# Dilated attention in an encoder block: values loaded and multiplied once per item, weights of both heads in one transfer, two buffers for the statistics' rows

## The chip, the cores and the metric

The kernel runs on one core of a Trainium2 chip. The metric is the device time of one execution in microseconds (us); before the change it is 1399.53 us, the median of three runs (1398.49 to 1399.57). The core has these engines, each with its own queue of instructions that it works through in order: PE (matmul, with PEld for its weight loads), DVE and ACT (elementwise work; they alone evacuate PE's results from PSUM), POOL (elementwise work in SBUF), and SP, which in this kernel issues nearly all transfers. The transfers themselves are carried by 16 DMA engines.

## The reference, cut to what matters

The block has three mixers. The change touches only the dilated attention: 24 heads in three groups of eight, with dilations 1, 4 and 16, and a softmax over the groups' log-denominators that weighs the three outputs of a head.

```python
A_GROUPS = ((128, 1), (512, 4), (2048, 16))
...
for gi, (window, dil) in enumerate(A_GROUPS):
    hs = slice(gi * A_HEADS, (gi + 1) * A_HEADS)
    o_g, lse_g = dilated_window_attention(aq[:, :, hs], ak[:, :, hs], av[:, :, hs], window, dil)
    outs.append(o_g)
    lses.append(lse_g)
wts = jax.nn.softmax(jnp.stack(lses, axis=0), axis=0).astype(dt)
oa = jnp.einsum('gbsh,gbshd->bshd', wts, jnp.stack(outs, axis=0)).reshape(b, s, BRANCH_WIDTH)
...
ya = (oa * jax.nn.silu(ga)) @ w_br_a[layer]
```

Inside a group a query sees a band of keys of its own residue class: 64 positions on either side for dilations 1 and 4, the whole class (64 positions) for dilation 16. There are 1024 tokens and 64 numbers per head.

## The kernel before

Everything before about 1060 us (projections, the other two mixers, rotary positions) leaves q, k and v of the dilated attention in device memory: `qkd` holds q and k with heads in pairs, `vdr` the values. The change lies in the stage that follows.

**Items and visits.** The eight heads of a group are worked in four pairs `p_`. An *item* is one pair in one group, so there are 12, in the order of `seq`: pair 0 with groups 0, 1, 2, then pair 1, and so on; items are counted from 0 in this document, so that item 5 is pair 1, group 2, and item 7 is pair 2, group 1. (Pair 0 has items 0 to 2.) The 1024 queries are eight tiles of 128, `T`, worked two at a time in four *visits* `b`. After each visit come two short steps `rest(T)` for `T` = 2b and 2b+1. An item is thus: visit 0, rest 0, rest 1, visit 1, rest 2, rest 3, visit 2, rest 4, rest 5, visit 3, rest 6, rest 7. The text calls these rests T0 to T7.

**What a visit does.** It computes on PE the scores of its two tiles (`scores`, L1567, L1571, L1579), on DVE the mask and the row minimum (L1591) and on ACT the exponential with its sum (`soft`, L1592). Two visits later PE transposes these probabilities (`trans`, L1614) and DVE copies them out of PSUM (L1620), so visits 0 and 1 of an item transpose tiles of the item before (`pre`). When half an item has been transposed, `pv` multiplies it with the values (L1635 for group 2, L1645 and, for the band's edges, L1655 for the others), and ACT moves the result into the tile `og` (L1665). This happens for `pre` in visits 0 and 2.

**Values.** `values(x)` loads one half of an item's values into the single tile `vfull` (named avs in the profile; L1516, L1520, L1524) right behind the `pv` that has read the item before out of that half. `turned_values` loads the copies with the other half of the partitions (avt; L1535, L1536, L1540) at T1. The last of them (L1536) exists because tile 4 of group 0 needs tile 3's values after that half has been overwritten.

**Statistics and weights.** In visit 1 `stats` turns the row minima and sums of `pre` (L1672) and ACT copies them to `sr` (one buffer; L1675, L1677, L1679); at T3 `send` writes them to device memory (`std`; L1687, L1691, L1694). When the three groups of a pair are done, `combine` puts 14 steps on the list `todo`; `STEP_T` says at which T each is taken, over the next three items: fetch the statistics (cpt, L1793), compute the shares, the weights, `put` them to `wgd` (L1818), load those of groups 0 and 1 back, broadcast over 64 partitions a head (`load`, wgt, L1788), multiply and add on POOL (`weigh`, L1826 and L1824), load group 2's and the gate (L1833), multiply and add, gate (L1829), store (L1837) or keep. This is done for pairs 0, 1 and 2: their `put` and first loads are at T3 of items 4, 7 and 10. Pair 3 is finished otherwise (`shares_3`, `ending`), from rows that are loaded at T2 and T4 of item 11 (L1727).

**Beside it.** Between the visits PE works on the y units (`add_y`, L1891): the gated output projections of the other two mixers. Their weights are loaded by SP (L1337), copied by ACT (L1342) and split on POOL (`y_split`, L1343); the gates' tiles come by L1350 and their evacuation is on DVE. The order on each engine is the order in which the program issues, and `weave` sets it from written costs that do not change here. Items 8 and 9 also load a finished part of the first branch (`dl_load`, hl, L1865, at T5), which ACT copies in the next item at T0 and T1 (`dl_high`, L1869).

**Buffers.** `vfull` has one, `wgt` two, `og` five, the probabilities (pra) five, their transposes (app) four, q and k two each. In PSUM the scores have two banks, transposes and `pv` and the statistics share four in rotation, the y units two.

Of the kernel before, what the change touches and what calls it, by code (L numbers as in the profile page):

```python
# [8 lines left out]
F32 = mybir.dt.float32  # L9
# [6 lines left out]
S = 1024  # L16
# [17 lines left out]
def block(ctx: ExitStack, tc: tile.TileContext, x, xT, memT, cst, msk, bcst, tabA, gpost,  # L34
# [174 lines left out]
    std = dram.tile([4, 3, 2, 2, S], F32, name="std")  # L209
    wgd = dram.tile([4, 2, 3, S], F32, name="wgd")  # L210
    tsd = dram.tile([4, 4, P, 512], F32, name="tsd")
# [1259 lines left out]
    with ExitStack():  # L1471
# [24 lines left out]
        def item(p_, g):  # L1496
# [5 lines left out]
            def place(T, h):  # L1502
                return h ^ (T // 2 % 2 if g == 2 else T % 2)

            def sides(T):
                return [not x for x in edges(g, T)]

            def values(x):

                v = vdr[g, p_]  # L1510
                if g == 2:
                    vv = v.rearrange("(u r) f -> u r f", r=16)
                    for o in range(2):
                        for h in range(2):
                            T = 4 * x + 2 * o
                            nc.sync.dma_start(vfull[hf[h ^ o], T:T + 2].rearrange("p b z d -> p (b z) d"),  # L1516
                                              vv[:, 2 * T:2 * T + 4, hf[h]])
                    return
                if g == 0:
                    nc.sync.dma_start(vfull[:, 4 * x:4 * x + 4].rearrange("p b h d -> p b (h d)"),  # L1520
                                      v[512 * x:512 * x + 512].rearrange("(b q) f -> q b f", q=128))
                else:
                    for e in range(2):
                        nc.sync.dma_start(vfull[:, 4 * x + e:4 * x + 4:2].rearrange("p b h d -> p b (h d)"),  # L1524
                                          v.rearrange("(u r) f -> u r f", r=4)[128 * e:128 * e + 128, 2 * x:2 * x + 2])

            def turned_values():

                v = vdr[g, p_]
                vturn = d["vt"] = aa.tile([P, 8, 64], F32, name="avt", bufs=2)  # L1530
                if g == 0:
                    vb_ = v.rearrange("(b k) f -> k b f", k=64)
                    for y, t0, t1, b0, h in ((0, 1, 8, 1, 1), (0, 2, 7, 3, 0), (1, 0, 7, 2, 1), (1, 1, 6, 4, 0)):
                        m = (t1 - t0 + 1) // 2
                        nc.sync.dma_start(vturn[hf[y], t0:t1:2], vb_[:, b0:b0 + 4 * m - 3:4, hf[h]])  # L1535
                    nc.sync.dma_start(vturn[hf[1], 7], v[448:512, hf[1]])  # L1536
                else:
                    vc = v.rearrange("(u r) f -> u r f", r=4)
                    for y in range(2):
                        nc.sync.dma_start(vturn[hf[y], 1 - y:8 - y:2], vc[64 + 64 * y:128 + 64 * y, :, hf[1]])  # L1540

            def value_of(T, h, side):

                y = place(T, h)
                vturn = d["vt"]
                if y == side:
                    return vturn[hf[y], T]
                if (g, T, side) == (0, 4, 0):
                    return vturn[hf[1], 7]
                return vfull[hf[y], T + (1 if side else -1), h]  # L1550
# [71 lines left out]

            def pv(b):
                if b == 0:
                    d["og"] = OG[p_, g] = cb.tile([P, S], F32, name="og", bufs=5)
                og = d["og"]
                ov = [pst().rearrange("p a b -> p (a b)") for _ in range(2)]
                if g == 2:
                    for j in range(2):
                        for z in range(2):  # L1630
                            for o in range(2):
                                T = 4 * b + 2 * o + j
                                for h in range(2):
                                    y, c = hf[place(T, h)], 128 * j + 64 * z
                                    PE.matmul(ov[o][hf[h], c:c + 64], vfull[y, T, z], st[T][y, z, 64 * j:64 * j + 64],  # L1635
                                              start=True, stop=True)
                    views = [(og.rearrange("p (u r) -> p r u", r=16)[:, 8 * b + 4 * o:8 * b + 4 * o + 4],
                              ov[o][:, 0:256].rearrange("p (r u) -> p r u", r=4)) for o in range(2)]
                else:
                    for i in range(2):  # L1640
                        for e in range(2):
                            T = 4 * b + 2 * i + e
                            for h in range(2):
                                c = 64 + 128 * e + 64 * place(T, h)
                                PE.matmul(ov[e][hf[h], 128 * i:128 * i + 128], vfull[:, T, h], st[T][:, :, c:c + 64],  # L1645
                                          start=i == 0, stop=False)
                    for i in range(2):
                        for r in range(2):
                            for e in range(2):
                                T = 4 * b + 2 * i + e  # L1650
                                if not sides(T)[r]:
                                    continue
                                for y in range(2):
                                    h, c = place(T, y), 128 * i + 64 * r
                                    PE.matmul(ov[e][hf[h], c:c + 64], value_of(T, h, r), st[T][hf[y], r, 320 * e:320 * e + 64],  # L1655
                                              start=False, stop=i == 1 and (r == 1 or not sides(T)[1]))
                    views = []
                    for e in range(2):
                        if g == 0:
                            dst = og[:, b * 512:b * 512 + 512].rearrange("p (i e q) -> p e i q", i=2, e=2)[:, e]  # L1660
                        else:
                            dst = og.rearrange("p (u r) -> p r u", r=4)[:, 2 * b:2 * b + 2, 128 * e:128 * e + 128]
                        views.append((dst, ov[e][:, 0:256].rearrange("p (i q) -> p i q", i=2)))
                for dst, src in views:
                    A.activation(dst, src, AF.Copy)  # L1665
                for T in range(4 * b, 4 * b + 4):
                    st.pop(T)

            def stats():
                sts = d["sts"]  # L1670
                tp = pst()
                PE.transpose(tp[0:32, 0, :], sts.rearrange("p h s t -> p (h s t)"), ident)  # L1672
                sr = cb.tile([32, 128], F32, name="sr", bufs=1)
                if g == 0:
# [26 lines left out]
        def plan(it, pre, nxt):  # L1701
# [77 lines left out]
        def combine(p_, ogs):  # L1779
# [5 lines left out]
            def load(g):  # L1785
                wgt[g] = cb.tile([P, S], F32, name="wgt", bufs=2)
                for h in range(2):
                    E.dma_start(wgt[g][h * 64:h * 64 + 64], wgd[p_, h, g:g + 1].to_broadcast([64, S]))  # L1788
# [27 lines left out]
            def put():  # L1816
                for h in range(2):
                    E.dma_start(wgd[p_, h].rearrange("g (i e) -> i g e", e=16), c["w"][h * 64:h * 64 + 64])  # L1818

# [530 lines left out]
```

## Time and profile before

The program was profiled in an execution of its own, which took 1399.23 us; its span, from the first to the last instruction, is 1397.1 us.

| what | before |
|---|---|
| median of 3 runs | 1399.53 us |
| profiled execution, its time and its span | 1399.23 us, 1397.1 us |
| issues of values (L1516, L1520, L1524) | 32, 8, 16 |
| issues of turned values (L1535, L1536, L1540) | 16, 4, 8 |
| issues of weights, shares, put (L1788, L1793, L1818) | 18, 6, 6 |
| `og` evacuations on ACT (L1665) | 48 of 128x256 |

How to read the profile: times are us from the start of the span. In the row of an engine on a page, busy time is followed by its share of the span and the number of instructions. A row of waits reads "who waited <- who ended the wait: us in total, times, longest us"; in a row of SP's own waits, SPq is its queue. A row of the timeline reads "start, duration, engine, line, operation, out<-in", and x4 at its end says that four alike were merged. A row of windows has, for each stretch, its length, the busy time of PE, PEld, DVE, ACT and POOL with the number of instructions, the granted share of PE's clock, the busy share of the 16 DMA engines and the GB/s that they moved. A group's row has "busy us, mean ns | idle time before it and what ended it". Tile names are the program's.

### The profile page before, as it was taken

Reading aid. Unit: us, or ns where it says so; the run is one execution under the profiler, and the core shown is the slowest. Engines: PE = TensorE matmul, PEld = TensorE weight load, DVE = VectorE, ACT = ScalarE, POOL = GpSimd, SP = SyncE. Lnnn points to the kernel's source line nnn. Section 1 sums busy time; section 2 is a strip of 40 time slices with the busy share of each in tenths; the row PEclk is TensorE's granted clock in tenths of the full one; section 3 lists DMA queues with packets and bytes.
Section 4 is the critical chain, followed back from the end, with each engine's and each line's share of the span. In section 5 each row is a group of like instructions: output and inputs, shape, how many; then the busy total and the mean of one; then the engine's idle time right before and its main releaser. Section 6 shows DMA issues by size and latency. Waiting matters only on the chain.

```text
span 1397.1 us, 22991 instructions
## 1 busy us (share of the span) xinstructions
PE 1365.4 (98%) x8303; PEld 1093.4 (78%) x8303; DVE 1016.2 (73%) x1840; ACT 658.2 (47%) x1408; POOL 579.4 (41%) x443
## 2 busy tenths in 40 slices
PE   7999999999999999999999999999999998899997
PEld 7799987666666789988888888888887776668886
DVE  7768667777776598767778776677777666568977
ACT  6454455656655345333333333433336775553332
POOL 0507702676666100245555553465651243552003
PEclk9999999999999999999999999999999999999999
DMA  6355532322243688424223333333338777876455
GB/s 234 103 183 199 186 114 99 101 77 91 75 139 135 216 249 251 156 83 128 92 98 113 117 110 111 117 121 113 105 128 275 218 199 209 243 198 218 142 198 181
DMA packets 126354, 213.88 MB, mean 153 GB/s; under 512 B 33345, under 2 KB 65441, under 8 KB 126241
## 3 DMA queue, kind: packets, MB, share of 16 engines
q1 hardware_dynamic: 116928, 198.49, 44.5%
q10 hardware_dynamic: 9312, 13.93, 2.8%
q8 instruction: 65, 1.06, 0.3%
q14 instruction: 49, 0.39, 0.1%
HBM read 145.99 MB, written 66.38 MB: 152 GB/s over the span
## 4 chain that ended last, share of the span: by engine, by line
PE 87%; DMA 4%; POOL 3%; DVE 2%; ACT 2%; issue 1%; SPq 1%; DVEq 0%; POOLq 0%; ACTq 0%
PE s L1309 35%; PE d L1891 5%; PE s L1219 4%; PE s L2115 4%; PE ov L804 4%; PE sc L2033 3%; PE d L128 3%; PE d L130 3%; PE d L132 3%; PE s L1270 3%; PE tr L770 2%; PE s L789 2%; PE s L788 2%; PE d L2115 2%; PE d L523 1%; DMA wgt<-wgd 1%
## 5 line engine op out<-in xcount | busy, mean ns | idle before, releaser
L795 POOL TENSOR_TENSOR bl<-bl,bp 128x512 f32<-128x512 f32 x96 | 133.0, 1385 | 54.1 <-ACT bp L791 48.6
L1309 PE MATMUL s<-hh,vS 128*128 128x512 f32 x400 | 133.4, 395 | 0.0
L1309 PE MATMUL s<-vA,vS 128*128 128x512 f32 x450 | 106.6, 390 | 0.0
L91 DVE TENSOR_TENSOR vS<-vot,vS 128x512 fp32r<-128x512 f32 x75 | 86.4, 1153 | 19.9 <-ACT vS L90 19.9
L1309 PEld LDWEIGHTS s<-vA,vS 128*128 128x128 f32 x450 | 84.5, 188 | 18.3
L791 ACT ACTIVATE bp<-s 128x512 f32<-128x512 f32 x128 | 75.7, 596 | 43.8 <-PE s L789 42.7
L771 DVE TENSOR_REDUCE bn<-tr 128x1 f32<-128x512 f32 x128 | 85.0, 684 | 13.7 <-PE tr L770 12.5
L128 PE MATMUL d<-hh,wh 128*128 128x512 f32 x224 | 90.1, 402 | 2.4 <-DVE fth L201 2.4
L1592 ACT ACTIVATE pra<-pra,sts 128x192 f32<-128x192 f32 (+1 forms) x176 | 72.8, 415 | 39.2 <-DVE sts L1591 39.0
L132 PE MATMUL d<-hh,wl 128*128 128x512 f32 x224 | 89.9, 402 | 0.0
L130 PE MATMUL d<-hl,wh 128*128 128x512 f32 x224 | 89.4, 399 | 0.0
L1309 PEld LDWEIGHTS s<-hh,vS 128*128 128x128 f32 x400 | 75.3, 188 | 17.7
L1620 DVE COPY app<-tr 128x320 f32<-128x320 f32 (+2 forms) x96 | 37.8, 435 | 59.1 <-PE tr L1614 59.1
L1309 PE MATMUL s<-hl,vS 128*128 128x512 f32 x200 | 79.1, 395 | 0.0
L1309 PE MATMUL s<-hh,wh 128*128 128x512 f32 x200 | 78.4, 392 | 0.0
L1309 PE MATMUL s<-hh,wl 128*128 128x512 f32 x200 | 78.4, 392 | 0.0
L1309 PE MATMUL s<-hl,wh 128*128 128x512 f32 x200 | 77.8, 389 | 0.0
L1313 ACT ACTIVATE vv<-s 128x512 f32<-128x512 f32 x50 | 30.0, 599 | 85.5 <-PE s L1309 59.0
L1053 POOL TENSOR_TENSOR vot<-wr 128x512 f32<-128x512 f32 x13 | 22.2, 1706 | 111.9 <-DMA wr<-in_wu 111.9
L804 PE MATMUL ov<-bp,VS 128*64 128x512 f32 x256 | 58.5, 598 | 0.0
L1053 POOL TENSOR_TENSOR vot<-vot,vA 128x512 f32<-128x512 f32 x12 | 19.3, 1609 | 90.6 <-DVE vS L91 90.6
L128 PEld LDWEIGHTS d<-hh,wh 128*128 128x128 f32 x224 | 42.6, 190 | 16.2 <-issue 5.5
(627 smaller groups left out, 4042.3 us busy)
## 6 DMA issues: line engine op xcount, KB each, us to landing
wr<-in_wu SPq DMA_DIRECT2D x40, 512.0 KB
vA<-in_wu SPq DMA_DIRECT2D x24, 512.0 KB
qkd<-ko SPq DMA_DIRECT2D x96, 128.0 KB
wl<-thd SPq DMA_DIRECT2D x24, 512.0 KB
wos<-os SPq DMA_DIRECT2D x12, 512.0 KB
wr<-in_wbr SPq DMA_DIRECT2D x24, 256.0 KB
aq<-qkd SPq DMA_DIRECT2D x12, 512.0 KB
ak<-qkd SPq DMA_DIRECT2D x12, 512.0 KB
```

What stands on the lines that cost most here:

```text
L91: V.tensor_tensor(dst_l, src, dst_h.bitcast(F32), op=OP.subtract)
L128: PE.matmul(dst, wh[:, k, :], hh[k][:, t], start=k == 0, stop=False)
L130: PE.matmul(dst, wh[:, k, :], hl[k][:, t], start=False, stop=False)
L132: PE.matmul(dst, wl[:, k, :], hh[k][:, t], start=False, stop=k == 7)
L771: fp["last"] = V.tensor_reduce(st[i]["n"][:, j, c:c + 1], s, axis=AX.X, op=OP.min)
L791: A.activation(pp, s, AF.Exp, scale=-1.0)
L795: G.tensor_tensor(lsum[i % 2], lsum[i % 2], pp, op=OP.add)
L804: PE.matmul(o[e * 64:e * 64 + 64], VS[:, kt, kv], d.pop(kt), start=kt < 2, stop=kt >= NT - 2)
L1309: PE.matmul(BANK[n, c], a, b, start=k == 0 and q == 0 and not more, stop=k == 3 and q == 2, skip_group_check=c in "XW")
L1592: A.activation(src, src, AF.Exp, scale=-1.0, bias=bias, accum_out=sts[:, 1, h, T:T + 1])
L1891: PE.matmul(ps_, a, b, start=k == 0 and q == 0, stop=k == 3 and q == 2)
L2115: PE.matmul(dst[:, e[0]:e[1]], a, b, start=k == 0 and q == 0, stop=k == 3 and q == 2)
```

## The change

- `pv` multiplies a whole item at once, in visit 2 of the next item, behind that visit's scores. Each PSUM bank then holds 512 columns, and `og` is evacuated by two instructions of 128x512 in place of four of 128x256. In group 2 the tiles are dealt to the two halves by T // 4.
- `values` loads a whole item at once, in visit 2, behind `pv`: one transfer for group 0, two for group 1, four for group 2. The extra turned tile is gone.
- In visits 0, 2 and 3 the transposes come behind the scores (in visit 2 also behind `pv`) and their copies behind the softmax on DVE; in visit 1 they stay ahead.
- `wgd` is laid out by group, then head. `load`, `fetch` and `put` use one transfer for both heads in place of one each.
- `STEP_T` moves eight of the 14 steps later, most by one T; the load of the gate goes from T1 to T4.
- `sr` has two buffers.

```diff
-    wgd = dram.tile([4, 2, 3, S], F32, name="wgd")
+    wgd = dram.tile([4, 3, 2, S], F32, name="wgd")
...
-                return h ^ (T // 2 % 2 if g == 2 else T % 2)
+                return h ^ (T // 4 if g == 2 else T % 2)
...
-            def values(x):
+            def values():
...
-                            T = 4 * x + 2 * o
-                            nc.sync.dma_start(vfull[hf[h ^ o], T:T + 2].rearrange("p b z d -> p (b z) d"),
-                                              vv[:, 2 * T:2 * T + 4, hf[h]])
+                            nc.sync.dma_start(vfull[hf[h ^ o], 4 * o:4 * o + 4].rearrange("p b z d -> p (b z) d"),
+                                              vv[:, 8 * o:8 * o + 8, hf[h]])
...
+                    nc.sync.dma_start(vfull.rearrange("p b h d -> p b (h d)"), v.rearrange("(b q) f -> q b f", q=128))
...
+                        nc.sync.dma_start(vfull[:, e:8:2].rearrange("p b h d -> p b (h d)"),
+                                          v.rearrange("(u r) f -> u r f", r=4)[128 * e:128 * e + 128])
...
-                    nc.sync.dma_start(vturn[hf[1], 7], v[448:512, hf[1]])
...
-                if (g, T, side) == (0, 4, 0):
-                    return vturn[hf[1], 7]
...
-            def pv(b):
+            def pv():
...
-                sr = cb.tile([32, 128], F32, name="sr", bufs=1)
+                sr = cb.tile([32, 128], F32, name="sr", bufs=2)
...
             def visit(b):
-                if pre and b in (0, 2):
-                    pre["pv"](b // 2)
                 at = it if b > 1 else pre
-                copies = at["trans"]((b + 2) % 4) if at and (it or b < 2) else []
+
+                def turning():
+                    return at["trans"]((b + 2) % 4) if at and (it or b < 2) else []
+
+                copies = turning() if b == 1 or not it else []
                 if it:
                     it["scores"](b)
+                if b == 2 and pre:
+                    pre["pv"]()
                 for f in copies:
                     f()
+                copies = turning() if b != 1 and it else []
                 if it:
                     it["soft"](2 * b)
                     it["soft"](2 * b + 1)
+                for f in copies:
+                    f()
...
-                if b in (0, 2):
-                    it["values"](b // 2)
+                if b == 2:
+                    it["values"]()
...
-                for h in range(2):
-                    E.dma_start(wgt[g][h * 64:h * 64 + 64], wgd[p_, h, g:g + 1].to_broadcast([64, S]))
+                E.dma_start(wgt[g], wgd[p_, g][:, None, :].to_broadcast([2, 64, S]))
...
-                for h in range(2):
-                    E.dma_start(c["t"][h * 64:h * 64 + 64].rearrange("p g s e -> p (g s) e"), std[p_, :, :, h].rearrange("g s (i e) -> i (g s) e", e=16))
+                E.dma_start(c["t"].rearrange("p g s e -> p (g s) e"), std[p_].rearrange("g s h (i e) -> (h i) (g s) e", e=16))
...
-                for h in range(2):
-                    E.dma_start(wgd[p_, h].rearrange("g (i e) -> i g e", e=16), c["w"][h * 64:h * 64 + 64])
+                E.dma_start(wgd[p_].rearrange("g h (i e) -> (h i) g e", e=16), c["w"])
...
-        STEP_T = (5, 0, 2, 3, 3, 6, 7, 0, 0, 1, 4, 5, 6, 7)
+        STEP_T = (5, 0, 2, 3, 3, 7, 0, 1, 1, 4, 5, 6, 7, 7)
```

More of the change, by code (lines that the diff above doesn't have):

```diff
@@ L1621, in trans @@
                 return [lambda: copy(0), lambda: copy(1)]
-            def pv(b):
-                if b == 0:
-                    d["og"] = OG[p_, g] = cb.tile([P, S], F32, name="og", bufs=5)
-                og = d["og"]
+            def pv():
+                og = OG[p_, g] = cb.tile([P, S], F32, name="og", bufs=5)
                 ov = [pst().rearrange("p a b -> p (a b)") for _ in range(2)]
                 if g == 2:
-                    for j in range(2):
+                    for j in range(4):
                         for z in range(2):
                             for o in range(2):
-                                T = 4 * b + 2 * o + j
+                                T = 4 * o + j
                                 for h in range(2):
-                                    y, c = hf[place(T, h)], 128 * j + 64 * z
-                                    PE.matmul(ov[o][hf[h], c:c + 64], vfull[y, T, z], st[T][y, z, 64 * j:64 * j + 64],
+                                    y, c, i = hf[place(T, h)], 128 * j + 64 * z, 64 * (j % 2)
+                                    PE.matmul(ov[o][hf[h], c:c + 64], vfull[y, T, z], st[T][y, z, i:i + 64],
                                               start=True, stop=True)
-                    views = [(og.rearrange("p (u r) -> p r u", r=16)[:, 8 * b + 4 * o:8 * b + 4 * o + 4],
-                              ov[o][:, 0:256].rearrange("p (r u) -> p r u", r=4)) for o in range(2)]
+                    views = [(og.rearrange("p (u r) -> p r u", r=16)[:, 8 * o:8 * o + 8],
+                              ov[o].rearrange("p (r u) -> p r u", r=8)) for o in range(2)]
                 else:
-                    for i in range(2):
+                    for i in range(4):
                         for e in range(2):
-                            T = 4 * b + 2 * i + e
+                            T = 2 * i + e
                             for h in range(2):
@@ L1646, in pv @@
                                           start=i == 0, stop=False)
-                    for i in range(2):
+                    for i in range(4):
                         for r in range(2):
                             for e in range(2):
-                                T = 4 * b + 2 * i + e
+                                T = 2 * i + e
                                 if not sides(T)[r]:
@@ L1655, in pv @@
                                     PE.matmul(ov[e][hf[h], c:c + 64], value_of(T, h, r), st[T][hf[y], r, 320 * e:320 * e + 64],
-                                              start=False, stop=i == 1 and (r == 1 or not sides(T)[1]))
+                                              start=False, stop=i == 3 and (r == 1 or not sides(T)[1]))
                     views = []
```

16 lines of the change are left out of this document (5 added, 11 removed).

## The prediction

> **What bounds the kernel now.** I read the page first, then the busy times by windows.
>
> ```profile
> span 1397.1 us, 22991 instructions
> PE 1365.4 (98%) x8303; PEld 1093.4 (78%) x8303; DVE 1016.2 (73%) x1840; ACT 658.2 (47%) x1408; POOL 579.4 (41%) x443
> ```
>
> ```profile
> 1200.00:1220.00 20.00, 15.56 (x220) 12.20 (x216) 8.73 (x35) 9.31 (x34) 10.98 (x6) 0.83 0.77 226
> ...
> 1240.00:1260.00 20.00, 16.59 (x178) 11.66 (x175) 10.86 (x42) 8.37 (x28) 15.09 (x8) 0.83 0.60 181
> ```
>
> ```profile
> 1180.00:1184.00 4.00, 4.00 (x62) 3.15 (x60) 2.07 (x11) 2.48 (x10) 0.00 (x0) 1.00 0.85 183
> ...
> 1204.00:1207.00 3.00, 0.00 (x0) 0.00 (x0) 0.00 (x0) 2.26 (x7) 3.00 (x2) 1.00 0.92 369
> ...
> 1060.00:1270.00 210.00, 197.35 (x2554) 151.17 (x2553) 134.62 (x581) 128.08 (x487) 84.32 (x41) 0.97 0.74 216
> ```
>
> PE is the bound. The dilated attention runs from about 1060 to 1270 us; in it PE is idle for 210 - 197.35 = 12.7 us. Two 20 us windows were granted 0.83 of the clock, so each lost 20 x 0.17 = 3.4 us. That makes 19.4 us in all that better feeding of PE could win here; the change adds and removes no matmul, so nothing else can be won. The last two figures of a window's row are the share in which the 16 DMA engines are busy and GB/s.
>
> The waits inside the stage say what the idle time is:
>
> ```profile
> POOL og L1826 <- DMA wgt<-wgd: 40.1, 6, 17.6
> ...
> PEld tr L1614 <- ACT sr L1679: 4.9, 2, 4.6
> ...
> ACT hh L1869 <- DMA hl<-od: 4.3, 1, 4.3
> ...
> PE s L1929 <- DMA rows<-std: 3.4, 1, 3.4
> ...
> PE d L1891 <- POOL wh L1343: 1.7, 2, 1.4
> ...
> PE tr L1645 <- DMA avs<-vdr: 1.3, 1, 1.3
> ```
>
> ```profile
> 1204.74 1.15 ACT L1869 ACTIVATE hh<-hl 128x512 fp32r<-128x512 f32 x2 [4.33 <-DMA hl<-od]
> ```
>
> Every one begins at a transfer that landed late: the values (avs), the rows of statistics, the first branch's output (hl: ACT waits 4.3 us for it, and PE behind ACT), and the weights (wgt), behind which POOL holds the split that the next y unit needs (L1343).
>
> SP, which issues all of these, is in order, and its own waits show why it is late:
>
> ```profile
> SPq L1837 <- POOL og L1829: 7.9, 2, 4.1
> ...
> SPq L1516 <- DMA wgt<-wgd: 3.9, 8, 0.7
> ```
>
> Its issues in item 7 and at the start of item 8 (line, then what is moved):
>
> ```profile
> 1177.53 1.26 SPq L1818 DMA_DIRECT2D wgd<-ceg  x2
> 1179.44 2.87 SPq L1788 DMA_DIRECT2D wgt<-wgd  x4
> 1182.41 1.05 SPq L1524 DMA_DIRECT2D avs<-vdr  x2
> 1183.51 0.45 SPq L1494 DMA_DIRECT2D aq<-qkd  x1
> 1184.01 0.42 SPq L1494 DMA_DIRECT2D ak<-qkd  x1
> 1184.53 0.39 SPq L1337 DMA_DIRECT2D wr<-in_wbr  x1
> 1185.02 0.38 SPq L1350 DMA_DIRECT2D wl<-thd  x1
> 1186.04 3.08 SPq L1516 DMA_DIRECT2D avs<-vdr  x4
> ```
>
> It stands at the store until POOL has gated, and values (L1516) wait for weights with which they share no data: in this order those weights stand eight issues ahead.
>
> **The change part by part.**
>
> *Unchanged work.* PE gets the same matmuls in another order. ACT evacuates two tiles of 128x512 in place of four of 128x256. Row:
>
> ```profile
> L1665 ACT ACTIVATE og<-tr 128x256 f32<-128x256 f32 x48 | 22.6, 555 | 17.3 <-PE tr L1655 12.6 <-PE tr L1635 4.7
> ```
>
> Between 0.55 us (no dearer by width) and 1.11 us (twice as dear) for each: 0 to 13 us less of ACT, which is idle for 210 - 128 = 82 us here. I take nothing. Transposes now stand behind the scores, their copies behind the softmax, and all of P times V behind the scores of visit 2; the two visits between a softmax and its transposes (some 6 us) cover that. If this cover failed, 12 items would lose up to the 1.1 us of one evacuation each.
>
> *Fewer issues.* Values: 56 transfers become 28; four of the turned values go; weights 18 to 9, shares 6 to 3, put 6 to 3. That is 47 issues less on SP, at about 0.5 us each (the rows above), and the eight-deep waits come less often. A second buffer for the statistics' rows ends a wait that no row above charges to PE: nothing. This part alone, and the later steps of the weighing, would give back most of the 19.4 us.
>
> *The merged load of weights.* Today each load of a group is two transfers, one per head: 64 rows that all repeat one row of 4 KB. The new one has a source of three dimensions: head (2), repeat (64, step 0), 1024 numbers.
>
> ```profile
> wgt<-wgd SPq DMA_DIRECT2D x18, 256.0 KB
> ```
>
> How many of the 16 engines get a share of such a transfer is shown by no row of before. One end: it is dealt out by its 128 target rows, all 16 engines work, and a load costs no more than today's pair. The other: it can only be dealt out in whole steps of the outermost dimension of both sides, the source's has two, and two engines carry 256 KB each. I take the second: source and target have to be cut alike, and the source has no cut finer than the head outside its repeat. Its price: at full tilt an engine moved 369 / 0.92 / 16 = 25.1 GB/s (window 1204 to 1207), so 262,144 bytes take **10.5 us** a load. The dear bound is the window 1180 to 1184, when hardly anything but weights flowed: 183 / 0.85 / 16 = 13.5 GB/s, 19.5 us. There 16 engines read the same row at once; here one engine reads each row, so I take the first.
>
> The Trainium skill speaks against the change here: "DMA: Bandwidth & Descriptors", section "Why a DMA increments its semaphore by 16 and not by 1", says that the engines used are the largest number up to 16 that divides the slowest dimension (not of size one) of both sides, as the instruction carries them; by it this load gets two, by the 128 target rows it would get 16. No view of before shows it for such a source. The same page's table of patterns advises one 128-partition transfer instead of two of halves; by that alone the load would cost what it does now.
>
> *What queues behind it.* Each engine takes SP's transfers in their order, and a transfer is done when its last engine is. So everything that SP issues after the loads waits for the two loaded engines, however idle the other 14 are. SP's order around the loads of the second pair stands above. The fixed cost of a small transfer, from the chain of waits:
>
> ```profile
> 1178.18 1.89 DMA wgd<-ceg
> ```
>
> Next behind the loads come the item's own values (L1524), which P times V needs one item later, in visit 2. Its PE rows in the three items that follow a load, the scores that will now stand before it, and SP's loads for the first and the third pair:
>
> ```profile
> 1142.11 1.09 PE L1645 MATMUL tr<-app,avs 128*64 128x128 f32 x16
> ```
>
> ```profile
> 1188.85 1.09 PE L1645 MATMUL tr<-app,avs 128*64 128x128 f32 x16
> ...
> 1190.27 0.34 PE L1614 MATMUL tr<-cs,pra 64*128 64x64 f32 x4
> 1190.54 0.46 PE L1567 MATMUL s<-ak,aq 64*64 64x64 f32 x16
> ```
>
> ```profile
> 1239.28 1.09 PE L1645 MATMUL tr<-app,avs 128*64 128x128 f32 x16
> ```
>
> ```profile
> 1132.19 3.26 SPq L1788 DMA_DIRECT2D wgt<-wgd  x4
> ```
>
> ```profile
> 1229.98 2.43 SPq L1788 DMA_DIRECT2D wgt<-wgd  x4
> ```
>
> Second pair: two loads from 1179.4, 1.9 us fixed, 2 x 10.5 us: the two engines are free at 1202.3; their share of the values takes about 2 us (512 KB / 16 / 25.1 GB/s is 1.3, short packets more): 1204.3. PE comes to these products at 1188.85, less 1.4 us for the half that no longer stands in visit 0 (half the products take 1188.85 to 1190.27), plus 0.5 us of scores: 1187.9. It waits 16.3 us. First pair, the same with 1132.2 and 1142.1: 15.8 us; third, with 1230.0 and 1239.3: 16.5 us. Sum **48.6 us** of new idle time. The waits of 4.6 and 3.4 us above lie in the two windows that lost 3.4 us of clock each; three longer ones cost **10.2 us** (0 if the clock holds).
>
> The third load of each pair is issued when the first weighing frees its buffer:
>
> ```profile
> L1826 POOL TENSOR_TENSOR og<-og,wgt 128x1024 f32<-128x1024 f32 x9 | 26.2, 2925 | 40.1 <-DMA wgt<-wgd 40.1
> ```
>
> At 1179.4 + 12.4 + 2.9 = 1194.7 it is issued, it queues on the two engines behind q, k and two more (1.75 MB / 16 / 25.1 = 4.6 us, to 1208.9) and ends at 1219.4; the load of hl behind it lands near 1223. ACT wanted it at 1204.74 - 4.33 = 1200.4 today, 11.5 us behind PE's products at 1188.85; with the slow clock (3.4) and the moved half (1.4) that is 16.3 us behind the restart, 1220.6: 3 to 5 us late. The same for the rows of statistics in the third pair (2 to 4 us), and for POOL's split behind the second weighing in the first (0 to 5). I take 10 us together, bounds 0 and 30.
>
> Today's 12.7 + 6.8 = 19.4 us are gone or are counted anew in these terms. **Sum:** the profiled execution took 1399.2 us (2.1 us around its span), which is within 0.3 us of the median of 1399.5; 1399.2 + 48.6 + 10.2 + 10 - 19.4 = **1449 us**.
>
> **The rivals.**
>
> *All 16 engines carry the merged load (faster).* Then SP has fewer issues and waits, nothing is slower, and the values get a whole item of lead. For it: a load of 128 whole rows, like aq and ak. Against it: the source's outermost dimension. The stalls on values and on POOL's split go, the wait for hl and for rows shrinks (the engines are 74% busy, so not to nothing; I leave 3 us of it, and one slow clock): 1399.2 - 19.4 + 3 + 3.4 = 1386 us.
>
> *Two engines, and the repeated row is what is slow.* 19.5 us a load: 18 us more before each first restart, 9 more behind each third load: 1449 + 3 x 27 = 1530 us. For it: the window at 183 GB/s. Against: that was 16 readers of one row.
>
> Today's weighing in the second pair, on POOL:
>
> ```profile
> 1184.68 5.81 POOL L1826 TENSOR_TENSOR og<-og,wgt 128x1024 f32<-128x1024 f32 x2 [17.59 <-DMA wgt<-wgd]
> 1190.46 1.28 POOL L1343 TENSOR_TENSOR wh<-wr,wh 128x512 fp32r<-128x512 f32 x1
> ```
>
> *Two engines, but others overtake.* If later transfers were done without the two engines, only POOL would be late: its first weighing would start at 1191.8 and not at 1184.7, and the split that PE needs is 7.1 us later, plus 3.4 us of clock, in each of three pairs: 1399.2 - 19.4 + 31.5 = 1411 us. Against it: each of those transfers has a share on every engine.
>
> *Nothing moves*, because the engines' bytes set the landing, not their number: 1399 us. Against it: 0.74 busy.
>
> **How the numbers follow.** Forecast 0.74, sixteen engines 0.14, the slow row 0.06, overtaking 0.04, no change 0.02. Less than 0.2% (2.8 us) can't be told from no change. So faster 0.14, same 0.02, slower 0.84. The forecast's own range is 1428 (the clock holds, no later stalls) to 1496 (later stalls at their bound, and a third of the way to the dear load: 1449 + 20 + 27). For 8 in 10 it takes in overtaking and no change below and some of the slow row above: 1395 to 1510.
>
> **What would show it.** Right: a few waits of PE's L1645 or L1655 for avs of 10 us or more, one in each of the three pairs (items 5, 8 and 11), windows there with a DMA share near 2/16 to 0.3 and under 100 GB/s, POOL's first weighing 10 us or more after its load was issued, and 0.8 clocks behind each. Wrong: weights landed within 6 us with a share near 1. A new wait of PE for ACT in visit 2 would refute the cost of nothing for the evacuation; stalls at the y units' L1891 alone would speak for overtaking.

## The result, and the profile after

The changed kernel takes 1468.29 us (median, 1468.14 to 1468.54) against 1399.55 us for the kernel before on the same chip: a ratio of 1.0491, 95% interval 1.0473 to 1.0509. That is 69 us slower. The profiled execution took 1468.4 us.

The page of after has the same matmuls in 69.5 us more of span. PE was busy 1375.3 us, 9.9 us more than before, and idle 1466.6 - 1375.3 = 91.3 us against 31.7 us, 59.6 us more. So most of the loss is waiting; the rest is the slower clock that the last windows below show:

```profile
span 1466.6 us, 22830 instructions
...
PE 1375.3 (94%) x8303; PEld 1102.6 (75%) x8303; DVE 1012.7 (69%) x1840; ACT 652.6 (44%) x1384; POOL 578.4 (39%) x443
```

The waits of after inside the stage (1060 to 1340 us):

```profile
POOL og L1821 <- DMA wgt<-wgd: 99.8, 9, 24.3
...
PE tr L1637 <- DMA avs<-vdr: 47.7, 5, 16.2
...
ACT hh L1864 <- DMA hl<-od: 10.1, 1, 10.1
...
PE s L1924 <- DMA rows<-std: 9.1, 1, 9.1
...
PE tr L1627 <- DMA avs<-vdr: 5.9, 4, 1.8
...
PE tr L1608 <- ACT sr L1670: 4.2, 1, 4.2
...
PE s L1565 <- DVE sts L1585: 3.2, 2, 2.1
```

POOL's wait for the weights (L1821 is `weigh`, L1826 before) went from 40.1 us to 99.8 us. PE's wait for values (L1637 is the `pv` of groups 0 and 1, L1645 before) went from 1.3 us to 47.7 us. PE's timeline shows it as three stops, each in visit 2 of the item behind the loads of a pair, in items 5, 8 and 11:

```profile
1156.36 0.69 PE L1637 MATMUL tr<-app,avs 128*64 128x128 f32 x4 [16.22 <-DMA avs<-vdr]
```

```profile
1225.08 0.69 PE L1637 MATMUL tr<-app,avs 128*64 128x128 f32 x4 [14.96 <-DMA avs<-vdr]
```

```profile
1296.90 4.04 PE L1637 MATMUL tr<-app,avs 128*64 128x128 f32 x32 [16.21 <-DMA avs<-vdr]
```

How the transfers run is read in SP's timeline, POOL's timeline and the windows around the first pair (in the windows the last three columns are PE's granted clock, the busy share of the 16 DMA engines, and GB/s):

```profile
1130.04 1.14 SPq L1785 DMA_DIRECT2D wgt<-wgd  x2
1131.27 9.03 SPq L1521 DMA_DIRECT2D avs<-vdr  x2
1140.39 10.97 SPq L1494 DMA_DIRECT2D aq<-qkd  x1
```

```profile
1144.52 2.85 POOL L1821 TENSOR_TENSOR og<-og,wgt 128x1024 f32<-128x1024 f32 x1 [8.39 <-DMA wgt<-wgd]
...
1155.73 2.86 POOL L1821 TENSOR_TENSOR og<-og,wgt 128x1024 f32<-128x1024 f32 x1 [7.14 <-DMA wgt<-wgd]
```

```profile
1132.00:1140.00 8.00, 8.00 (x114) 6.03 (x110) 6.03 (x32) 6.41 (x30) 2.39 (x1) 1.00 0.13 48
1144.00:1152.00 8.00, 0.00 (x0) 0.00 (x0) 0.00 (x0) 0.00 (x0) 4.07 (x2) 0.50 0.13 52
1156.00:1160.00 4.00, 3.48 (x32) 2.98 (x32) 0.00 (x0) 0.00 (x0) 3.92 (x2) 0.54 0.48 180
1176.00:1181.00 5.00, 4.60 (x75) 3.76 (x75) 1.84 (x7) 2.98 (x8) 4.92 (x3) 0.66 0.78 303
1193.00:1198.00 5.00, 4.35 (x44) 4.26 (x46) 2.90 (x15) 2.00 (x9) 0.00 (x0) 0.66 0.53 174
1225.00:1231.00 6.00, 5.75 (x69) 4.79 (x70) 0.37 (x5) 0.62 (x1) 4.73 (x2) 0.50 0.26 95
1245.00:1255.00 10.00, 5.70 (x75) 4.38 (x75) 2.78 (x8) 6.51 (x21) 8.20 (x4) 0.50 0.91 325
1297.00:1303.00 6.00, 5.91 (x70) 4.85 (x71) 0.63 (x6) 0.83 (x1) 4.61 (x2) 0.50 0.16 58
1310.00:1323.00 13.00, 6.20 (x54) 4.21 (x58) 3.59 (x13) 0.41 (x2) 8.73 (x4) 0.50 0.61 192
```

While the weights flow, the DMA engines are 0.13 busy, and 2/16 is 0.125. PE stands still for eight microseconds beside 14 idle engines. The first weighing starts 14.5 us after its load's issue, the second 11.2 us later: that is what a load takes, 262,144 bytes for one engine in 11.2 us, or 23.4 GB/s. SP itself is held at its issues too, 9.0 us for the two of the values and 11.0 us for q. The lower rows show the half clock behind each stop, up to 6 us long after PE had restarted, and again behind the later, shorter waits.

### The profile page after: what moved, and what is told of

Same layout as the page of the kernel before. It is cut to its first block, busy times and chain, and to the rows that moved or that the text cites. A ratio compares the mean times of both kernels' runs of the same rounds, so it can differ in the third digit from the quotient of the medians.

```text
span 1466.6 us, 22830 instructions
## 1 busy us (share of the span) xinstructions
PE 1375.3 (94%) x8303; PEld 1102.6 (75%) x8303; DVE 1012.7 (69%) x1840; ACT 652.6 (44%) x1384; POOL 578.4 (39%) x443
## 4 chain that ended last, share of the span: by engine, by line
PE 80%; DMA 8%; POOL 3%; DVE 3%; ACT 2%; SPq 2%; issue 1%; DVEq 0%; POOLq 0%; ACTq 0%
PE s L1309 33%; DMA wgt<-wgd 5%; PE s L1219 4%; PE d L1886 4%; PE s L2110 4%; PE ov L804 3%; PE sc L2028 3%; PE s L1270 3%; PE d L130 3%; PE d L128 3%; PE d L132 3%; PE tr L770 2%; PE s L789 2%; PE s L788 2%; PE d L2110 2%
## 5 line engine op out<-in xcount | busy, mean ns | idle before, releaser
L1585 DVE CUSTOM_DVE_ANT_0 pra<-s,mask 128x192 f32<-128x192 f32 (+1 forms) x192 | 49.8, 309 | 125.9 <-PE tr L1608 91.3
L1637 PE MATMUL tr<-app,avs 128*64 128x128 f32 x256 | 22.1, 337 | 47.8 <-DMA avs<-vdr 47.7
L1821 POOL TENSOR_TENSOR og<-og,wgt 128x1024 f32<-128x1024 f32 x9 | 25.7, 2853 | 99.8 <-DMA wgt<-wgd 99.8
L1657 ACT ACTIVATE og<-tr 128x512 f32<-128x512 f32 x24 | 20.2, 926 | 87.8 <-PE tr L1647 56.1
```

## The experiments

All ratios are against the kernel before, run on the same chip beside each; its medians were between 1399.1 and 1400.6 us. Differences between kernels are taken from the ratios, times 1399.5 us; by the intervals they are good to some 3 us.

| kernel | median us | ratio (95%) |
|---|---|---|
| changed | 1468.3 | 1.0491 (1.0473 to 1.0509) |
| changed, weights in two transfers | 1394.1 | 0.9948 (0.9933 to 0.9963) |
| before, weights merged | 1474.6 | 1.0521 (1.0503 to 1.0539) |
| changed, source of 4 rows | 1433.8 | 1.0237 (1.0220 to 1.0254) |
| changed, source of 8 rows | 1427.2 | 1.0185 (1.0169 to 1.0200) |
| rows stored four times, two transfers | 1405.9 | 1.0045 (1.0029 to 1.0061) |
| only the first two loads merged | 1447.1 | 1.0342 (1.0322 to 1.0361) |
| only the third load merged | 1416.6 | 1.0126 (1.0110 to 1.0141) |
| first two merged, on ScalarE's queue | 1451.3 | 1.0376 (1.0356 to 1.0396) |
| two transfers, old order in a visit | 1393.5 | 0.9955 (0.9943 to 0.9966) |
| two transfers, rows loaded earlier | 1388.8 | 0.9920 (0.9907 to 0.9934) |
| the last, and shares later | 1391.2 | 0.9936 (0.9922 to 0.9951) |
| before, small parts alone | 1398.7 | 0.9992 (0.9981 to 1.0003) |

**The load alone, undone and done.** The first takes the merged load out of the changed kernel, the second puts it alone into the kernel before.

```diff
-                E.dma_start(wgt[g], wgd[p_, g][:, None, :].to_broadcast([2, 64, S]))
+                for h in range(2):
+                    E.dma_start(wgt[g][h * 64:h * 64 + 64], wgd[p_, g, h:h + 1].to_broadcast([64, S]))
```

> The changed kernel with only the load of weights put back to two transfers, one per head (64 rows each); all else as changed. If the two loaded DMA engines are the cause, the three waits of PE for the values (47.4 us together), the later waits and the slow clock behind them go, and the rest of the change shows what it is worth: about 1386 us, not above 1400 us. If the values in one visit, the new order of transposes and copies or the wider evacuations cost something of their own, it stays above 1410 us.

```diff
-                for h in range(2):
-                    E.dma_start(wgt[g][h * 64:h * 64 + 64], wgd[p_, h, g:g + 1].to_broadcast([64, S]))
+                E.dma_start(wgt[g], wgd[p_, :, g][:, None, :].to_broadcast([2, 64, S]))
```

> The kernel before with only the load of weights merged into one transfer per group; all else as before. If the two engines are the whole cause: PE waits for values by 10 us or more behind each of the three pairs' loads, and the time is 1445 to 1480 us. If the merged load hurts only together with values that are loaded and multiplied in one visit, it stays below 1415 us.

With two transfers the kernel takes 1394.1 us, with the merged load the old kernel takes 1474.6 us. In ratios, the load costs 0.0543 in the new surroundings and 0.0521 in the old ones: 76 and 73 us. In the old kernel with the merged load, PE stops for the values too:

```profile
PE tr L1645 <- DMA avs<-vdr: 52.2, 4, 18.5
```

So values loaded whole, the new order and the wider evacuations are not needed for the loss, and without the load the rest is 0.5% faster than before. Page, waits (1060 to 1345 us) and windows of the changed kernel with two transfers:

```profile
span 1392.0 us, 22853 instructions
...
PE 1362.6 (98%) x8303; PEld 1093.2 (79%) x8303; DVE 1012.6 (73%) x1840; ACT 652.9 (47%) x1384; POOL 579.0 (42%) x443
```

```profile
PE s L1925 <- DMA rows<-std: 4.7, 1, 4.7
...
PE s L1565 <- DVE sts L1585: 3.7, 2, 2.6
```

```profile
1133.00:1138.00 5.00, 5.00 (x61) 3.78 (x59) 3.97 (x21) 5.00 (x22) 3.41 (x2) 1.00 1.00 246
```

No wait of PE for values is left. The same 4 KB rows, each repeated 64 times, now come with a share of 1.00 at 246 GB/s (the window also holds the values behind them) instead of 0.13 at 48. But PE is idle 1392.0 - 1362.6 = 29.4 us, only 2.3 us less than before the change: it still waits for the rows (3.4 us before, 4.7 us now), and a wait for DVE's `sts` is new. The two waits together, 8.4 us, are about what the time lies above the expected 1386.

**How many engines.** Each row is stored two or four times, so that the source's outermost dimension is 4 or 8 (here the edit for 4):

```diff
-    wgd = dram.tile([4, 3, 2, S], F32, name="wgd")
+    wgd = dram.tile([4, 3, 2, 2, S], F32, name="wgd")
...
-                E.dma_start(wgt[g], wgd[p_, g][:, None, :].to_broadcast([2, 64, S]))
+                E.dma_start(wgt[g], wgd[p_, g].rearrange("h r s -> (h r) s")[:, None, :].to_broadcast([4, 32, S]))
...
-                E.dma_start(wgd[p_].rearrange("g h (i e) -> (h i) g e", e=16), c["w"])
+                for r in range(2):
+                    for h in range(2):
+                        E.dma_start(wgd[p_, :, h, r].rearrange("g (i e) -> i g e", e=16), c["w"][h * 64:h * 64 + 64])
```

> The changed kernel with each row of weights stored twice, so that the merged load's source has 4 as its outermost dimension (4 rows, each repeated 32 times); three small issues more in each pair. If the outermost dimension sets the number of engines: 4 engines with 128 KB each, 5.2 us a load in place of 10.5, each first wait of PE 10 us shorter (about 6 us), 1400 to 1430 us. If a repeated row is slow whatever the number of engines, or the merged form itself is, it stays within 10 us of 1468 us.

> As with four rows, but each row of weights stored four times: 8 rows, each repeated 16 times; seven small issues more in each pair. If the outermost dimension sets the number of engines: 8 engines, 64 KB each, 2.6 us a load; no first wait of PE above 3 us is left: 1385 to 1402 us. If not, within 10 us of 1468 us.

The control stores the rows four times as well, and loads with two transfers of 64 rows:

> The control for the kernels with rows stored twice and four times: each row stored four times (seven small issues more in each pair), but loaded in two transfers of 64 rows as in the split kernel. If these issues only delay the loads by some 6 us and the slack covers it: 1393 to 1402 us, and the 33 us that the kernel with 8 rows lies above the split one are the load's. If the issues themselves cost: 1415 us or more.

The two weighings of the first pair with 4 rows, and a window of that kernel in which hardly anything but weights flows; below them the weighings with 8 rows, and a window of that kernel:

```profile
1142.91 2.85 POOL L1823 TENSOR_TENSOR og<-og,wgt 128x1024 f32<-128x1024 f32 x1 [6.87 <-DMA wgt<-wgd]
...
1151.05 2.85 POOL L1823 TENSOR_TENSOR og<-og,wgt 128x1024 f32<-128x1024 f32 x1 [4.08 <-DMA wgt<-wgd]
```

```profile
1135.50:1137.50 2.00, 2.00 (x17) 1.42 (x17) 1.17 (x8) 1.68 (x9) 0.54 (x1) 1.00 0.26 86
```

```profile
1143.17 2.85 POOL L1823 TENSOR_TENSOR og<-og,wgt 128x1024 f32<-128x1024 f32 x1 [7.02 <-DMA wgt<-wgd]
...
1148.99 2.86 POOL L1823 TENSOR_TENSOR og<-og,wgt 128x1024 f32<-128x1024 f32 x1 [1.75 <-DMA wgt<-wgd]
```

```profile
1142.00:1148.00 6.00, 0.00 (x0) 0.00 (x0) 0.00 (x0) 0.00 (x0) 4.07 (x2) 0.50 1.08 168
```

With 4 rows the share is 0.26: four of 16 engines. With 8 rows it is 0.46 from 1137 to 1139 us, when the load has just begun: near eight. A load takes 8.1 us by the two weighings, with 8 rows 5.8 us, against 11.2 us with 2. So the number of rows in the outermost dimension sets the number of engines, and the kernel's time falls with it: 69 us above the kernel before, then 33, then 26, with three and seven small issues more. A load's time falls by less than half at each step: the 5.2 us expected for 4 rows and the 2.6 us for 8 were both wrong, and both kernels lie above what was expected (1400 to 1430 and 1385 to 1402 us). In the last window above all 16 engines are busy with 168 GB/s, 10.5 GB/s each: the values and q, held back no longer, run at the same time, and it seems that they slow one another. The control says that seven more issues cost some 14 us by themselves (0.0097), more than expected, so of 8 rows' 33 us above the two transfers the load's own part is about 20 us. Why one engine among 16 busy ones moves less than half of what it moves alone was not tried.

**Which load costs what.** One of the branches is `g < 2` (the first two loads merged, the third in two transfers), the other `g == 2`:

```diff
-                E.dma_start(wgt[g], wgd[p_, g][:, None, :].to_broadcast([2, 64, S]))
+                if g < 2:
+                    E.dma_start(wgt[g], wgd[p_, g][:, None, :].to_broadcast([2, 64, S]))
+                else:
+                    for h in range(2):
+                        E.dma_start(wgt[g][h * 64:h * 64 + 64], wgd[p_, g, h:h + 1].to_broadcast([64, S]))
```

> The changed kernel, but the third load of each pair (the one issued when the first weighing frees its buffer) goes as two transfers; the first two stay merged. If the three waits for values come from the first two loads: they stay at about 16 us each, and of the later waits (24 us) and their slow clock most go: 1438 to 1452 us. If the third load is what hurts: below 1425 us.

> The opposite: only the third load is merged, the first two go as two transfers each. By the same theory the 16 us waits are gone, and one late load of 10.5 us is left in each pair, behind which later transfers come some 5 us late: 1398 to 1415 us. With the run above this splits the loss into its two terms; if both are far above what they should be, the loads' prices don't add.

PE's waits for transfers in the kernel with the first two merged, then in the one with the third:

```profile
PE tr L1637 <- DMA avs<-vdr: 52.8, 6, 18.8
```

```profile
PE s L1928 <- DMA rows<-std: 10.3, 1, 10.3
...
PE tr L1608 <- ACT sr L1670: 6.0, 1, 6.0
PE tr L1627 <- DMA avs<-vdr: 5.7, 4, 2.9
```

The two losses nearly add up. Over the kernel with two transfers, the first two loads cost 0.0394 (55 us), the third 0.0178 (25 us), and all three 0.0543 (76 us). The first two make the waits of `pv` and nothing else of size; the third makes the waits for the rows, for hl (behind which ACT copies `sr` late) and for group 2's values. The third load alone came out just above the 1398 to 1415 us expected.

**Queue or engines.** The first two merged loads go to ScalarE's queue of transfers (`nc.scalar.dma_start` in the first branch above), so SP's own transfers no longer stand behind them in one queue.

> The changed kernel, the first two loads merged as they are, but issued on ScalarE's queue of transfers and not on SP's; the third in two parts on SP. If values are late because they stand behind the weights in the same queue on the two loaded engines: PE's first waits fall to under 6 us each and the time to 1395 to 1425 us, though POOL still waits 10 us or more for the weights. If the two engines are simply taken, whatever the queue, PE's first waits stay above 10 us and the time above 1435 us.

PE's waits in that kernel, and SP's own waits; then the load's issue on ACT's queue and the weighing on POOL:

```profile
PE s L1928 <- DMA rows<-std: 19.3, 1, 19.3
...
PE d L1890 <- POOL wh L1343: 14.7, 3, 10.5
...
PE tr L1627 <- DMA avs<-vdr: 10.4, 7, 6.0
...
PE tr L1637 <- DMA avs<-vdr: 3.0, 1, 3.0
```

```profile
SPq L1789 <- DMA wgt<-wgd: 43.7, 3, 15.6
```

```profile
1130.40 1.63 ACTq L1786 DMA_DIRECT2D wgt<-wgd  x2
```

```profile
1149.74 2.90 POOL L1825 TENSOR_TENSOR og<-og,wgt 128x1024 f32<-128x1024 f32 x1 [11.33 <-DMA wgt<-wgd]
```

Half of each expectation came true. The first waits are gone (3.0 us are left of 47.7), so the values were indeed late because they stood behind the weights in the same queue. Whether they stood in line at the two engines or in SP, which was held at its issues, is not told apart: in this kernel SP issues the values in 1.2 us. But the time is 1451 us, 60 us above the kernel with two transfers and no better than with the same two loads on SP's queue (1447 us). The weights land later still (the first weighing starts 19.3 us after the issue), as is to be expected if they share the two engines with SP's transfers. Two things stand behind them. SP stands 43.7 us at the third load, whose buffer the first weighing holds, and the rows come late behind it. And POOL, which works in order, does the split of the y units' weights (L1343) only after the weighing. This is the second pair, where PE's longest wait for a split (10.5 us) ends:

```profile
1216.04 2.85 POOL L1825 TENSOR_TENSOR og<-og,wgt 128x1024 f32<-128x1024 f32 x1 [31.50 <-DMA wgt<-wgd]
1218.85 1.26 POOL L1343 TENSOR_TENSOR wh<-wr,wh 128x512 fp32r<-128x512 f32 x1
```

The stop moved; the two engines' work did not get less.

**What the rest is worth.** Four kernels without the merged load. The order in a visit is put back as before:

```diff
-                copies = turning() if b == 1 or not it else []
-                if it:
-                    it["scores"](b)
                 if b == 2 and pre:
                     pre["pv"]()
-                for f in copies:
-                    f()
-                copies = turning() if b != 1 and it else []
+                copies = turning()
+                if it:
+                    it["scores"](b)
+                for f in copies:
+                    f()
+                copies = []
```

> The split kernel with the old order in a visit: P times V ahead of the scores, the transposes ahead of the softmax everywhere. If the new order costs nothing and gains little, within 3 us of the split kernel (1391 to 1397 us). If the new order is what hides the evacuations and copies, waits of PE for DVE or ACT appear in visits 0 to 2 and the time is above 1400 us; if the new order is what makes PE wait for DVE (2.6 and 1.1 us in the split kernel), it is below 1391 us.

It makes no difference (0.9955 against 0.9948). The statistics' rows for the last pair go ahead of the last item's values on SP:

```diff
-                    if T in (2, 4):
-                        j = T // 4
-                        nc.sync.dma_start(rows[32 * j:32 * j + 32], std[3, j].rearrange("s h (t a) -> (s h t) a", t=NT))
+                    if T == 2:
+                        row_load(0)
+
+            def row_load(j):
+                nc.sync.dma_start(rows[32 * j:32 * j + 32], std[3, j].rearrange("s h (t a) -> (s h t) a", t=NT))
...
+                if b == 2 and seq.index(it["key"]) == 11:
+                    row_load(1)
                 if b == 2:
                     it["values"]()
```

> The split kernel with the second load of the statistics' rows for the last pair issued ahead of the last item's values on SP. If PE's wait of 4.7 us for these rows is due to the place in SP's order, it goes and takes one slow clock with it: 1387 to 1390 us. If something else ends there at the same time: no change from the split kernel's 1394 us.

PE's waits left in it, in the same stretch:

```profile
PE s L1565 <- DVE sts L1585: 2.9, 2, 1.8
...
PE tr L1608 <- ACT sr L1670: 2.1, 1, 2.1
```

The wait for the rows is gone, and the kernel is the fastest of all, 1388.8 us, 0.8% below the kernel before. By the ratios it is 4 us below the one with two transfers, whose interval its own just touches. Next, the shares (the second of the weighing's steps) go from T0 to T1:

```diff
-        STEP_T = (5, 0, 2, 3, 3, 7, 0, 1, 1, 4, 5, 6, 7, 7)
+        STEP_T = (5, 1, 2, 3, 3, 7, 0, 1, 1, 4, 5, 6, 7, 7)
```

> As the last one, and the first step of the weighing on VectorE (the shares) three microseconds later (one half visit), since in the split kernel VectorE stood 2.0 us for their transfer and PE 2.6 us behind it. If that wait is what holds PE: 2 to 4 us below the last one, 1383 to 1387 us. If the later weights make POOL's split late instead: no better than the last one.

No better (1391.2 us, the intervals overlap): PE's wait for `sts` is still there, 3.5 us in two. But DVE's wait for the shares' transfer is still there as well (1.8 us, and 1.3 us in the kernel with only the rows moved), so the edit did not take away what it was meant to. Only the longer of the two waits for `sts` has such a wait of DVE ahead of it; whether that one comes from the transfer stays open. Last, the kernel before with `fetch` and `put` merged, two `sr`, and nothing else:

> The kernel before with only the small parts of the change that leave the values and the order alone: statistics' rows doubled, the fetch of shares and the storing of weights in one transfer each, weights loaded in two transfers as before. If the gain of the split kernel over the one before (6 us) comes from fewer issues on SP in general: part of it, 1395 to 1398 us. If it comes from the values loaded whole: no difference from before, 1398 to 1401 us.

No difference (0.9992, 0.9981 to 1.0003). So the 0.5% comes from what is left: values loaded and multiplied whole with the wider evacuations, or the weighing's new due times. Which of these was not tried.

## Why the prediction was right, and where not

**The load and its first price: right.** Two engines (share 0.13, and 0.26 with four rows), 10.5 us a load against 11.2 measured, and the first load landing 14.5 us after its issue against the 12.4 of the prediction. By the Trainium skill, "DMA: Bandwidth & Descriptors", section "Why a DMA increments its semaphore by 16 and not by 1", two and four engines were due; the shares of 0.13 and 0.26 agree. The Trainium skill's advice in the same page's section "Rules for kernel authors", one transfer of 128 partitions in place of two of halves, would by itself have kept the load's cost; here the one transfer cost 76 us more than the two, and the measurement decides.

**The first waits: right.** 48.6 us predicted, 16.22 + 14.96 + 16.21 = 47.4 measured, in the named items. The picture behind it was not complete: SP was held 9.0 us at the values' two issues, which the prediction had put at 1.1 us. The waits came out alike because either way they end when the two engines are through: in all three pairs PE restarts 0.5 to 0.6 us after the second weighing starts (1156.36 after 1155.73, 1225.08 after 1224.52, 1296.90 after 1296.41). There is a little luck in the closeness. In the first pair PE restarted 26.3 us after the loads' issue, where 24.8 were reckoned, but it also arrived 10.1 us after it, where 9.0 were reckoned, and the two errors nearly cancel.

**The clock behind them: nearly right.** 10.2 us predicted. By the windows (share of the clock lost, times PE's busy time) it is 0.46 x 3.48 + 0.50 x 5.75 + 0.50 x 5.91 = 7.4 us.

**The third load and later waits: mis-sized.** "I take 10 us together, bounds 0 and 30". By the runs the third load cost 21 us (changed kernel less the one with two merged) to 25 us (third alone less two transfers). Three things were left out. The values of group 2 are queued behind it too (5.9 us). The rows came 9.1 us late, not 2 to 4. (hl came 10.1 us late for ACT, not 3 to 5; only 4.2 us of it reached PE, so its price fits although its lateness does not.) And these waits have half clocks of their own: 0.34 x 4.60 + 0.34 x 4.35 + 0.50 x 5.70 + 0.50 x 6.20 = 9.0 us in the four windows at 1176, 1193, 1245 and 1310 us. The prediction had charged the clock to the first waits alone. For before, it had taken the lost share over whole windows, PE's idle time included (6.8 us). Reckoned as here, it is 0.46 x 7.00 + 0.46 x 5.52 = 5.8 us, from these windows of the kernel before:

```profile
1208.00:1215.00 7.00, 7.00 (x72) 5.55 (x72) 4.47 (x14) 2.60 (x10) 1.86 (x1) 0.54 0.81 196
...
1249.00:1256.00 7.00, 5.52 (x43) 3.58 (x46) 3.55 (x13) 0.41 (x2) 6.01 (x4) 0.54 0.66 238
```

The slow clock thus cost 7.4 + 9.0 - 5.8 = 10.6 us more than before, near the 9.9 us by which PE was busy longer.

**The 19.4 us to be won back: the step that failed most.** The prediction took all of "today's 12.7 + 6.8 = 19.4 us" off and expected that fewer issues "would give back most" of them. The kernel without the merged load won 0.0052, 7 us. Of the two long waits of before, the one behind hl (4.6 us) went, but the one for the rows stayed (3.4 us before, 4.7 us now), and one for `sts` came (3.7 us). So there are still two stretches at half clock, and by these windows of that kernel they cost 0.48 x 7.00 + 0.45 x 6.34 = 6.2 us, no less than the 5.8 us of before:

```profile
1170.00:1177.00 7.00, 7.00 (x106) 6.48 (x105) 1.94 (x9) 1.12 (x6) 0.00 (x0) 0.52 0.41 109
...
1242.00:1249.00 7.00, 6.34 (x78) 4.35 (x78) 3.59 (x13) 0.41 (x2) 3.12 (x2) 0.55 0.58 216
```

The six issues saved by `fetch` and `put` were worth nothing where they were tried alone; those of the values were not tried alone. The rows' wait was a matter of SP's order: with their load moved ahead, it went.

In all, the terms measured against the kernel before are -7 for the rest, +55 for the first two loads, +21 for the third: 69 us, against -19.4, +58.8 and +10: 49.4 us. Two errors of the same sign make the 19 us by which 1449 was too low.

**The rivals.** "Sixteen engines" (1386 us) describes the kernel with two transfers, which took 1394.1. The slow repeated row (19.5 us a load) is refuted by the 11.2 us that a load took. The 246 GB/s of the same row in two transfers would not refute it: over 16 engines that is 15.4 GB/s each, not far from the 13.5 of that rival. "Overtaking" (1411 us) was not what happened. A second queue comes nearest to it: its sign, PE waiting for POOL's split, did appear there, but not alone, and the kernel took 1451 us. The evacuations cost nothing, as taken: an instruction of 128x512 took 0.93 us in place of two of 0.55, ACT was busy 652.6 us after 658.2, and none of PE's waits above in visit 2 is for ACT's `og`.

```profile
L1657 ACT ACTIVATE og<-tr 128x512 f32<-128x512 f32 x24 | 20.2, 926 | 87.8 <-PE tr L1647 56.1
```

## What to carry to other kernels

Look at the outermost dimension of both sides of every transfer: two transfers of 64 equal rows used all engines, one of 2 x 64 used two, and it held everything behind it in its queue. When a transfer is late, follow the queue it is in and then the buffer it holds: taking it to another queue moved the wait here and did not shorten it. A saving of idle time is won only after the next late transfer has been looked for; here, 7 of 19 us.

## What the runs showed of the hardware

- A sequencer is held at the issue when the few engines of its queue are loaded: 9.0 us for two issues and 11.0 us for one on SP with two engines; 5.8 us with four, in the SP row below (q, kernel with 4 rows). With the two loads on ACT's queue, SP issued the same two values in 1.2 us. What decides how much is taken ahead was not tried.

```profile
1138.61 5.81 SPq L1494 DMA_DIRECT2D aq<-qkd  x1
```

- One of two engines that ran almost alone moved 23.4 GB/s (11.2 us for 256 KB); with 8 rows and all 16 busy, one moved 10.5 GB/s on weights and other tiles (168 GB/s over the core).
- After a stop of 15 to 16 us PE ran at half its clock for 3 to 6 us more. Shorter waits had half clocks behind them too: after one of 2.1 us (for `sts`, up to 1193.65 us) the window from 1193 to 1198 us shows 0.66, and between waits of 1.0 and 4.2 us the clock stood at 0.50 from 1245 to 1255 us, with PE busy for 5.7 of these ten microseconds.
